# Attention on one core: power and cube of VectorE's exponentials added by a DMA into one tile, two value terms in place of three

## The chip, the core and the metric

The kernel runs on one core of one Trainium2 chip. The metric is device time in microseconds (us) of one execution. The engines are named as in the profile: PE (TensorE's matmuls) and PEld (its weight loads), DVE (VectorE), ACT (ScalarE), POOL (GpSimd), SP (SyncE, which only issues DMAs here). Each takes its instructions in the order in which they were written, and waits at the first one whose data isn't there.

## The reference

Multi-query attention: 8 batches, 1024 positions, 16 heads of 64 for the queries, and one head of keys and values that all 16 share.

```python
scores = np.matmul(q, k.transpose(0, 1, 3, 2)) / np.sqrt(head_dim)
weights = np.exp(scores - np.max(scores, axis=-1, keepdims=True))
weights = weights / np.sum(weights, axis=-1, keepdims=True)
attn_out = np.matmul(weights, v)
```

The kernel subtracts no maximum. It divides by the sum at the end: a column of constants stands beside the 64 columns of v, so the value matmul gives the sum of weights as its 65th column.

## The kernel before

**Units.** The work is cut into 1024 units. A unit is one pair of heads, one half (512) of the queries and one chunk of 128 keys: 128 partitions (keys) x 2 heads x 512 queries = 128x1024 exponentials. Eight units in a row (all keys of one pair and half) make a block; there are 128 blocks.

**Scores.** `scores` writes a unit's 128x1024 scores with two matmuls into one of three PSUM tiles (`sc`). Keys are scaled so that a score is 1024 times the exponent of two.

**Two ways to the exponentials.** Most units (800, kind "A") go to ACT: `scalar_exp`, one activation, fp16 out into one of 22 tiles (`wt`). The others (224, kind "V") go to DVE, which makes the exponential out of the bits of an fp16 number, in a tile `w3` (in the profile `we`) of three parts of 128x1024:

- `ve_bits` adds the exponent's offset to the score and stores it as int16. Read as fp16, part 1 is the power of two times (1 + fraction), a straight line between powers.
- `ve_mantissa` cuts the mantissa out (m, between 1 and 2); `ve_power` cuts the exponent out into part 0; `ve_square` makes m squared; the product of part 1 and m squared, the cubic piece, goes to part 2. POOL makes the first columns of it (`ve_cube`), DVE the others (`ve_rest`).

The exponential is a sum of the three parts with fixed factors. The sum is never made in the tile: `prep_v` keeps three copies of v (in `vp`), with the factors 1, C0 and C3, and the value matmuls add the three terms in PSUM.

**Values.** A block has 16 groups (4 x 128 queries, 2 heads). For each group, `value` multiplies each unit's weights (128x128, loaded as PE's weights) with v (128x65). `terms_of` gives the order in a group: first one term of all 8 units, then the further terms of the V units. Seven groups share a PSUM bank (`ot`); when it is full, DVE takes the reciprocal of the sums (`inverse`), multiplies (`finish`), and SP stores.

`check` tests the sums' range; where one were outside, a second, general program would run after (it doesn't with these inputs).

**Order.** `plan` writes out the order of everything by hand. It keeps a clock for each engine with fixed costs (`T_MM` for a value matmul, `T_ACT` for an activation, `VE_COST` for DVE's), and a time at which each term is `ready`; it emits scores when a PSUM tile is free, values in between, chooses the kind of each unit, and splits each cube between POOL and DVE. `DEFER`, `REST`, `MINC`, `NEXT`, `LATE`, `VE_SLACK` and `NEAR` steer these choices. Only the order reaches the chip. POOL also issues the casting loads of q and v (`load_q`, `load_v`); SP issues q's transposes (`turn_q`) 20 scores later.

Of the kernel before, what the change touches and what calls it, by code (L numbers as in the profile page):

```python
# [11 lines left out]
FP16 = mybir.dt.float16  # L12
I32 = mybir.dt.int32
I16 = mybir.dt.int16
ALU = mybir.AluOpType
# [3 lines left out]

SUM_LO = 128.0  # L20
SUM_HI = 60000.0
C0 = 0.9833984375
C3 = 0.163818359375
CS = 2.1471603163479376
N_WT = 22
N_W3 = 8
N_M = 2
N_M2 = 3
T_PAIR = 214.0
T_IN = 96.0  # L30
T_OUT = 106.0
T_MM = 29.6
T_SCORE = 480.0
T_ACT = 917.0
ACT_DONE = 1110.0
MM_DONE = 270.0
VE_TAIL = 115.0
# [3 lines left out]
GP_COL = 1.887  # L41
GP_TAIL = 230.0
T_LOAD = {"load_q": 640.0, "load_v": 1000.0}
SIDE = (("prep_k", 58), ("prep_v", 72))
VE_COST = {
    "bits": 1141.0,
# [8 lines left out]
    "finish": 542.0,  # L55
}
ORDER = {"bits": 0, "inverse": 1, "finish": 2}
NEXT = {"bits": 0.0, "inverse": 0.0, "finish": 0.0}
MINC = 128
REST = 768  # L60
LATE = 500.0
VSLOT = 1
DEFER = 12
HOLD = 1400.0
VE_SLACK = 2500.0
V_END = 12
RATE = 0.235
NEAR = 2000.0
WAIT = -100.0
T_BITS = 1255.0  # L70
SAFE = 300.0


@with_exitstack
def attention_main(ctx, tc, q, k, v, out, flag):
# [11 lines left out]
    nc = tc.nc  # L87
    B, S, H, D = q.shape
    P = 128
    NKT = S // P  # L90
# [13 lines left out]
    consts = ctx.enter_context(tc.tile_pool(name="consts", bufs=1))  # L104
# [12 lines left out]
    ident16 = consts.tile([P, P], FP16, name="ident16")  # L117
    ones = consts.tile([P, 1], FP32, name="ones")
    rec_all = consts.tile([P, NG], FP32, name="rec_all")
    vps = [consts.tile([P, 3, NKT, 72], FP16, name=f"vp{i}") for i in range(2)]  # L120
    ok_all = consts.tile([P, B + GRP], FP32, name="ok_all")
    qf = consts.tile([P, NKT, P], FP32, name="qf")

# [1 line left out]
    ve = {}  # L125
# [5 lines left out]
    wt = {}  # L131
# [115 lines left out]

    def prep_v(b):
        vp = kv[b]["vp"]
        for i, ci in ((1, C0), (2, C3)):  # L250
            x = nc.vector.tensor_scalar(  # L251
                out=vp[:, i, :, 0:D], in0=vp[:, 0, :, 0:D], scalar1=ci, scalar2=None, op0=ALU.mult
            )
        return x
# [23 lines left out]
    def ve_bits(u, i):  # L278
        p, c, j = where(u)
        w3 = w3p.tile([P, 3, 2, QCH], FP16, tag=f"w3_{i}", name=f"we{p}_{c}_{j}")  # L280
        wt[u] = [(w3[:, 1], 0), (w3[:, 0], 1), (w3[:, 2], 2)]
        ve[u] = {"w3": w3}
        nc.vector.tensor_scalar(  # L283
            out=w3[:, 1].bitcast(I16),
            in0=sc.pop(u),
            scalar1=15.0 * 1024,
            scalar2=0.0,
            op0=ALU.add,
            op1=ALU.max,
        )  # L290

    def ve_mantissa(u, i):
        ve[u]["m"] = mp.tile([P, 2, QCH], FP16, tag=f"m{i}", name=f"m{u}")
        return nc.vector.tensor_scalar(  # L294
            out=ve[u]["m"].bitcast(I16),
            in0=ve[u]["w3"][:, 1].bitcast(I16),
            scalar1=0x3FF,
            scalar2=0x3C00,
            op0=ALU.bitwise_and,
            op1=ALU.bitwise_or,  # L300
        )

    def ve_power(u):
        return nc.vector.tensor_scalar(  # L304
            out=ve[u]["w3"][:, 0].bitcast(I16),
            in0=ve[u]["w3"][:, 1].bitcast(I16),
            scalar1=0x7C00,
            scalar2=None,
            op0=ALU.bitwise_and,
        )  # L310

    def ve_square(u, i):
# [18 lines left out]
    def after_vector(x, key):  # L331
        tc.add_manual_dep(
            x.ins,
            made[key].ins.name,
            mybir.DependencyInfo(mybir.DependencyClass.Sync, mybir.DependencyReason.DATA),
            reason="GpSimd reads beside VectorE's next pass over PSUM",
        )

    def cube_of(u):
        w3 = ve[u]["w3"]  # L340
# [119 lines left out]
    kinds = {}  # L460

    def terms_of(h):
        us = range(h * NKT, (h + 1) * NKT)
        own = [(u, 0) for u in us]
        return own + [(u, i) for i in (1, 2) for u in us if kinds[u] == "V"]

    def plan():
        ops = []
# [4 lines left out]
        t_pe = t_ve = t_act = t_gp = 0.0  # L473
        mode = "v"
        u = 0
# [3 lines left out]
        ready = {}  # L479
# [5 lines left out]
        m2_used = [0.0] * N_M2  # L485
# [5 lines left out]
        behind = None  # L491
        t_behind = 0.0
        loads = []
        live = {}
        h = g = n = 0
        terms = None
# [25 lines left out]
        def share(s):  # L522

            nonlocal t_gp, lock, behind
            if behind is None:
                return
            v = next((v for v in left if left[v]), None)
            if v is not None:
                gs = max(t_gp, t_behind + GP_START, squared[v] + GP_START)
                n = min(int((s - gs - GP_FIX) / GP_COL) // 32 * 32, left[v])  # L530
                if n >= MINC:
                    lo = 2 * QCH - left[v]
                    emit(gs, "cube", v, lo, lo + n, behind)
                    left[v] -= n
                    lock = gs + GP_FIX + n * GP_COL
                    t_gp = lock + GP_TAIL
                    ready[v, 2] = max(ready.get((v, "g"), 0.0), t_gp)
                    ready[v, "g"] = ready.pop((v, 2))
                    for x in loads:
                        emit(t_gp, *x)  # L540
                        t_gp += T_LOAD[x[0]]
                    loads.clear()
            behind = None

        def vector_step(limit):

# [3 lines left out]
            for x in [(r, "bits", v, 0) for v, r in todo] + evict:  # L550
                r, what = x[:2]
                s = max(t_ve, r, min(w3_used) if what == "bits" else 0.0)
# [14 lines left out]
            if not urgent and (  # L567
                chain or left and (flush or left[next(iter(left))] <= REST or u - next(iter(left)) > DEFER)
            ):
                what, v = chain[0] if chain else ("rest", next(iter(left)))  # L570
                old = next(iter(left), None)
                if old is not None and (
                    left[old] <= REST
                    or what == "square"
                    and min(m2_used) == float("inf")
                    or u - old > DEFER
                ):
                    what, v = "rest", old
                s = t_ve
                if what == "mantissa":  # L580
                    s = max(s, ready[v, 0], min(m_used))
                elif what == "square":
                    s = max(s, live["s", v], min(m2_used))
                elif what == "rest":
                    s = max(s, squared[v] + VE_TAIL)
                if s >= limit:
                    return False
                share(s)
                s = max(s, lock)
                if what == "rest":  # L590
                    n = left.pop(v)
                    done = 0.0
                    if n:
                        emit(s, "rest", v, 2 * QCH - n)
                        t_ve = s + VE_FIX + n / 1.92
                        done = t_ve + VE_TAIL
                        behind, t_behind = ("rest", v), t_ve
                    ready[v, 2] = m2_used[live.pop(("m2", v))] = max(done, ready.get((v, "g"), 0.0))
                    return True
                chain.pop(0)  # L600
                t_ve = s + VE_COST[what]
                if what in ("prep_k", "prep_v", "check"):
                    emit(s, what, v)
                    behind, t_behind = (what, v), t_ve
                    return True
                done = t_ve + VE_TAIL
                behind, t_behind = (what, v), t_ve
                if what == "mantissa":
                    live["m", v] = hold(m_used, s)[0]
                    live["s", v] = done  # L610
                    emit(s, what, v, live["m", v])
                elif what == "power":
                    emit(s, what, v)
                    ready[v, 1] = done
                else:
                    m_used[live.pop(("m", v))] = done
                    live["m2", v] = hold(m2_used, s)[0]
                    emit(s, what, v, live["m2", v])
                    left[v] = 2 * QCH
                    squared[v] = t_ve  # L620
                return True
            if best is None or best[1] >= limit:
                return False
            _, s, x = best
            r, what, g0, nn = x
            if what == "bits":
                v = g0
# [3 lines left out]
                t_ve = s + VE_COST["bits"]  # L631
# [64 lines left out]
        while h < H or u < STEPS:  # L696
            guard += 1
            assert guard < 400000

            while vector_step(t_pe):  # L700
                pass
# [55 lines left out]
            idle += 20.0  # L757
        while vector_step(float("inf")):
            pass
        assert u == STEPS  # L760
        return [(what, args) for _, _, what, args in sorted(ops, key=lambda x: x[:2])]

# [18 lines left out]
    with tc.manual_schedule():  # L781
# [6 lines left out]
        for c in range(NKT):  # L788
            load_q(0, c)
        for t in vps:  # L790
            for i, ci in enumerate((1.0, C0, C3)):
                nc.gpsimd.memset(t[:, i, :, D : D + 1], ci)
        nc.vector.tensor_copy(out=ident16, in_=ident)
        nc.vector.memset(ones, 1.0)
# [13 lines left out]
        for c in range(NKT):  # L808
# [6 lines left out]
            "power": ve_power,  # L815
            "square": ve_square,
            "cube": ve_cube,
            "rest": ve_rest,
            "load_q": load_q,
            "load_v": load_v,  # L820
# [140 lines left out]
```

## Time and profile before

| | |
|---|---|
| median of 3 runs | 762.9 us (762.39 to 763.02) |
| profiled execution, its own time | 762.94 us |
| its span, first to last instruction | 761.1 us |
| granted PE clock, mean | 0.997 |
| DMA, mean | 97 GB/s |

The profile gives one execution. Busy time is a union of rows, and rows of one engine overlap: an activation's row takes 1046 ns on average while 800 of them take 745.0 us together. So what an instruction costs its engine is read from the distance between starts, and what an engine lacks from the idle time before its groups. Matmul ends are modelled.

### The profile page before, as it was taken

The page shows a single profiled execution, that of the slowest core. Times are in us where ns is not written, and L with a number is a line of the kernel's source. Part 1 is how long each engine was busy: PE and PEld are TensorE (multiplying, and loading weights), DVE is VectorE, ACT ScalarE, POOL GpSimd, SP SyncE. Part 2 cuts the span into 40 slices and gives each one's busy share as a digit, 9 for nine tenths or more (in the row PEclk, how much of TensorE's full clock was granted, in tenths as well). Part 3 has the DMA queues.
Part 4 walks back from the last instruction along what each step waited for, and adds up shares of the span by engine and source line. Part 5 has one row for each costly group of instructions (what it writes and reads, how often), then busy time and mean ns, then how long its engine had stood idle before and what let it go on. Part 6 is the DMA issues. An engine that isn't in the chain of part 4 may idle for free.

```text
span 761.1 us, 31746 instructions
## 1 busy us (share of the span) xinstructions
PE 746.3 (98%) x13858; PEld 480.7 (63%) x13858; DVE 728.8 (96%) x1474; ACT 747.5 (98%) x803; POOL 327.2 (43%) x364
## 2 busy tenths in 40 slices
PE   6999999999999999999999999999999999999996
PEld 3566666666666666666666666666666665666665
DVE  4999999999999999999999999999999999999994
ACT  7999999999999999999999999999999999999995
POOL 4644444443444344543444344434444334444440
PEclk9999999999999999999999999999999999999999
DMA  9964437663466525665446563467535565211112
GB/s 173 167 121 99 99 64 114 113 117 94 78 118 113 105 62 112 106 113 92 79 93 112 114 113 74 90 111 125 99 75 95 100 112 96 71 44 58 30 58 73
DMA packets 168926, 73.91 MB, mean 97 GB/s; under 512 B 94032, under 2 KB 161616, under 8 KB 168784
## 3 DMA queue, kind: packets, MB, share of 16 engines
q1 hardware_dynamic: 149152, 53.76, 32.7%
q0 software_dynamic: 18576, 17.57, 18.3%
q8 instruction: 109, 1.79, 1.1%
q10 hardware_dynamic: 1056, 0.52, 0.2%
q14 instruction: 33, 0.27, 0.1%
HBM read 37.75 MB, written 33.55 MB: 94 GB/s over the span
## 4 chain that ended last, share of the span: by engine, by line
ACT 54%; PE 42%; issue 3%; DMA 1%; DVE 1%
ACT wt L276 54%; PE ot L396 24%; PE sc L263 17%; DMA knat<-in_k_dram 0%; PE otl L420 0%; DMA out_dram<-osb 0%; DVE osb L354 0%; PE kps L200 0%; PE qps L216 0%; DVE k L191 0%; DVE rec_all L345 0%; DVE k2t L212 0%; PE cnt L837 0%; DVE okm L835 0%; DVE ok_all L443 0%
## 5 line engine op out<-in xcount | busy, mean ns | idle before, releaser
L276 ACT ACTIVATE wt<-sc 128x1024 f16<-128x1024 f32 x800 | 745.0, 1046 | 1.1 <-PE sc L263 0.9
L319 POOL TENSOR_TENSOR we<-we,mm 128x448 f16<-128x448 f16 (+4 forms) x279 | 281.9, 1010 | 409.2 <-DVE mm L315 214.4
L396 PE MATMUL ot<-vp,wt 128*128 128x65 f16 x6336 | 432.2, 194 | 0.0
L396 PE MATMUL ot<-vp,we 128*128 128x65 f16 x5376 | 432.2, 194 | 0.0
L396 PEld LDWEIGHTS <-wt 128*128 128x128 f16 x6336 | 317.4, 97 | 115.0 <-issue 115.0
L396 PEld LDWEIGHTS <-we 128*128 128x128 f16 x5376 | 316.1, 97 | 104.5 <-issue 103.4
L263 PE MATMUL sc<-qt,k2t 64*128 64x512 f16 x2048 | 354.3, 385 | 4.4 <-ACT wt L276 2.9
L283 DVE TENSOR_SCALAR we<-sc 128x1024 int16<-128x1024 f32 x224 | 272.5, 1217 | 8.7 <-PE sc L263 6.7
L315 DVE TENSOR_TENSOR mm<-m 128x1024 f16<-128x1024 f16 x224 | 151.8, 678 | 0.0
L263 PEld LDWEIGHTS <-k2t 64*128 64x128 f16 x2048 | 80.1, 93 | 48.5 <-issue 7.8
L294 DVE TENSOR_SCALAR m<-we 128x1024 int16<-128x1024 int16 x224 | 92.5, 413 | 0.2
L304 DVE TENSOR_SCALAR we<-we 128x1024 int16<-128x1024 int16 x224 | 92.5, 413 | 0.0
L354 DVE TENSOR_TENSOR osb<-ot,rec_all 128x448 f32<-128x448 f32 x146 | 89.2, 611 | 0.2
L327 DVE TENSOR_TENSOR we<-we,mm 128x576 f16<-128x576 f16 (+7 forms) x222 | 87.4, 394 | 0.0
L166 POOL DMA_DIRECT2D q<-in_q_dram x64 | 38.6, 606 | 5.5 <-issue 1.5
L345 DVE RECIPROCAL rec_all<-ot 128x7 f32<-128x7 f32 x146 | 28.7, 197 | 7.4 <-PE ot L396 6.8
L149 POOL DMA_DIRECT2D vp<-in_v_dram x8 | 7.2, 899 | 0.0
L251 DVE TENSOR_SCALAR vp<-vp 128x512 f16<-128x512 f16 x16 | 3.8, 279 | 2.2 <-DMA vp<-in_v_dram 2.2
L200 PE MATMUL kps<-ident,k 128*64 128x128 f16 x16 | 1.3, 314 | 4.4 <-DVE k L191 4.3
L234 DVE TENSOR_SCALAR k16d<-knat 128x1024 f16<-128x1024 f32 x7 | 4.7, 672 | 0.0
L229 DVE COPY qt<-qps 128x512 f16<-128x512 f16 (+1 forms) x2 | 1.1, 555 | 3.0 <-PE qps L216 3.0
L200 PEld LDWEIGHTS <-k 128*64 128x64 f16 x16 | 0.8, 158 | 4.6 <-DVE k L191 4.6
(30 smaller groups left out, 23.7 us busy)
## 6 DMA issues: line engine op xcount, KB each, us to landing
out_dram<-osb SPq DMA_DIRECT2D x109, 256.0 KB, 2.6
q<-in_q_dram POOLq DMA_DIRECT2D x56, 256.0 KB, 4.4
out_dram<-osb SPq DMA_DIRECT2D x38, 128.0 KB, 2.4
knat<-in_k_dram SPq DMA_DIRECT2D x7, 256.0 KB, 3.9
q<-in_q_dram POOLq DMA_DIRECT2D x8, 192.0 KB, 8.2
vp<-in_v_dram POOLq DMA_DIRECT2D x8, 128.0 KB, 5.8
qt<-q SPq DMA_TRANSPOSE x64, 4.8
qf<-in_q_dram ACTq DMA_DIRECT2D x2, 256.0 KB, 4.0
```

The lines of the kernel that those rows point to most:

```text
L166: nc.gpsimd.dma_start(out=q16[(b, c)], in_=q[b, c * P : (c + 1) * P, h0:, :].rearrange("p h d -> p (h d)"),)
L263: nc.tensor.matmul(sc[u][:, hh, :], k2t[r : r + 64, j * P : (j + 1) * P], qt[b][r : r + 64, p % HP, c * QCH : (c + 1) * QCH], start=True, ...
L276: nc.scalar.activation(out=w, in_=sc.pop(u), func=EXP, scale=escale, bias=math.log(CS))
L283: nc.vector.tensor_scalar(out=w3[:, 1].bitcast(I16), in0=sc.pop(u), scalar1=15.0 * 1024, scalar2=0.0, op0=ALU.add, op1=ALU.max,)
L294: return nc.vector.tensor_scalar(out=ve[u]["m"].bitcast(I16), in0=ve[u]["w3"][:, 1].bitcast(I16), scalar1=0x3FF, scalar2=0x3C00, op0=ALU.b ...
L304: return nc.vector.tensor_scalar(out=ve[u]["w3"][:, 0].bitcast(I16), in0=ve[u]["w3"][:, 1].bitcast(I16), scalar1=0x7C00, scalar2=None, op0 ...
L315: return nc.vector.tensor_tensor(out=ve[u]["m2"], in0=m, in1=m, op=ALU.mult)
L319: x = nc.gpsimd.tensor_tensor(out=wu[:, lo:hi], in0=we[:, lo:hi], in1=mm[:, lo:hi], op=ALU.mult)
L327: return nc.vector.tensor_tensor(out=wu[:, lo:], in0=we[:, lo:], in1=mm[:, lo:], op=ALU.mult)
L345: nc.vector.reciprocal(out=rec_all[:, g0 : g0 + n], in_=o[:, 0:n, D])
L354: nc.vector.tensor_tensor(out=ob[:, i0 : i0 + n, :], in0=o[:, 0:n, 0:D], in1=rec.unsqueeze(2).broadcast_to([P, n, D]), op=ALU.mult,)
L396: nc.tensor.matmul(ots[g0][:, gg - g0, 0 : D + 1], w[:, hh, qb * P : (qb + 1) * P], kv[h // (HP * NCH)]["vp"][:, ci, u % NKT, 0 : D + 1], ...
```

## The change

Parts 0 and 2 get the same factor, so that they can be added. The mantissa is cut out with exponent bits 0x3800 in place of 0x3C00 (m between a half and 1, so the cube is a quarter of what it was); the power gets two low bits set (0x0201) by a second operation of the same instruction. A new step, `merge`, issues a DMA from POOL that adds part 0 into part 2 within SBUF. Value terms of a V unit are then part 1 with v times KAPPA, and part 2 with v. `prep_v` makes one scaled copy of v, not two.

`plan` gets the step: a merge is due when power, rest and cube are done, costs POOL 650 ns (`T_MERGE`), and its term is ready 5000 ns after its start (`MERGED`). Several of the planner's costs and choices have other values too. In the built order 220 units go to DVE and 804 to ACT.

```diff
-C0 = 0.9833984375
-C3 = 0.163818359375
-CS = 2.1471603163479376
+KAPPA = 1.5258396029178207
+CS = 3.2766468288976904
-T_PAIR = 214.0
+T_PAIR = 215.5
-T_OUT = 106.0
-T_MM = 29.6
+T_OUT = 120.0
+T_MM = 30.2
-T_ACT = 917.0
+T_ACT = 905.0
+T_MERGE = 650.0
+MERGED = 5000.0
+TERMS = (2,)
-NEXT = {"bits": 0.0, "inverse": 0.0, "finish": 0.0}
-MINC = 128
-REST = 768
-LATE = 500.0
+NEXT = {"bits": 100.0, "inverse": 0.0, "finish": 60.0}
+MINC = 256
+REST = 640
+LATE = 2500.0
-DEFER = 12
+DEFER = 6
-VE_SLACK = 2500.0
+VE_SLACK = 1800.0
-NEAR = 2000.0
+NEAR = 200.0
-SAFE = 300.0
+SAFE = 0.0
-    vps = [consts.tile([P, 3, NKT, 72], FP16, name=f"vp{i}") for i in range(2)]
+    vps = [consts.tile([P, 2, NKT, 72], FP16, name=f"vp{i}") for i in range(2)]
...
-        for i, ci in ((1, C0), (2, C3)):
+        for i, ci in ((1, KAPPA),):
...
-        wt[u] = [(w3[:, 1], 0), (w3[:, 0], 1), (w3[:, 2], 2)]
+        wt[u] = [(w3[:, 1], 1), None, (w3[:, 2], 0)]
...
-            scalar2=0x3C00,
+            scalar2=0x3800,
...
-            scalar2=None,
+            scalar2=0x0201,
             op0=ALU.bitwise_and,
+            op1=ALU.bitwise_or,
...
+    def merge(u):
+        w3 = ve[u]["w3"]
+        nc.gpsimd.dma_start(out=w3[:, 2], in_=w3[:, 0], accum_op=ALU.add)
...
-        return own + [(u, i) for i in (1, 2) for u in us if kinds[u] == "V"]
+        return own + [(u, i) for i in TERMS for u in us if kinds[u] == "V"]
...
+        def merge():
+            nonlocal t_gp
+            done, v = merges.pop(0)
+            s = max(t_gp, done)
+            emit(s, "merge", v)
+            t_gp = s + T_MERGE
+            ready[v, 2] = s + MERGED
...
-                    ready[v, 2] = m2_used[live.pop(("m2", v))] = max(done, ready.get((v, "g"), 0.0))
+                    done = max(done, ready.get((v, "g"), 0.0), ready[v, 1])
+                    m2_used[live.pop(("m2", v))] = done
+                    merges.append((done, v))
...
+            while merges and max(t_gp, merges[0][0]) < min(t_pe, t_ve):
+                merge()
...
-            for i, ci in enumerate((1.0, C0, C3)):
+            for i, ci in enumerate((1.0, KAPPA)):
```

More of the change, by code (lines that the diff above doesn't have):

```diff
@@ L493, in plan @@
         loads = []
+        merges = []
         live = {}
@@ L759, in plan @@
             pass
+        while merges:
+            merge()
         assert u == STEPS
@@ L817, in attention_main @@
             "cube": ve_cube,
+            "merge": merge,
             "rest": ve_rest,
```

## Prediction

> **What bounds the kernel now.** I read the totals, the groups by line, the waits, then the timeline of PE and the chain of waits.
>
> ```profile
> span 761.1 us, 31746 instructions
> PE 746.3 (98%) x13858; PEld 480.7 (63%) x13858; DVE 728.8 (96%) x1474; ACT 747.5 (98%) x803; POOL 327.2 (43%) x364
> ...
> L276 ACT ACTIVATE wt<-sc 128x1024 f16<-128x1024 f32 x800 | 745.0, 1046 | 1.1 <-PE sc L263 0.9
> L396 PE MATMUL ot<-vp,wt 128*128 128x65 f16 x6336 | 432.2, 194 | 0.0
> L396 PE MATMUL ot<-vp,we 128*128 128x65 f16 x5376 | 432.2, 194 | 0.0
> L263 PE MATMUL sc<-qt,k2t 64*128 64x512 f16 x2048 | 354.3, 385 | 4.4 <-ACT wt L276 2.9 <-DVE we L283 0.8
> ```
>
> Three engines are within 4% of the span, so busy shares don't choose. The idle column does: PE never waits before a value matmul, and 4.4 us before all scores. The timeline of PE shows what its time is made of (start, length, group, count):
>
> ```profile
> 403.88 0.39 PE L263 MATMUL sc<-qt,k2t 64*128 64x512 f16 x2
> 404.20 0.20 PE L396 MATMUL ot<-vp,wt 128*128 128x65 f16 x1
> ...
> 404.70 0.19 PE L396 MATMUL ot<-vp,we 128*128 128x65 f16 x1
> 404.83 0.39 PE L263 MATMUL sc<-qt,k2t 64*128 64x512 f16 x2
> ```
>
> 17 values start between 404.20 and 404.70 (31 ns apart), the next score 0.13 us later, the first value 0.32 us after a score. Over the trace from 15 us on, starts lie 31.1 ns apart from value to value (10963 times), 130 from value to score (741), 315 from score to value (741), 223 from one unit's score to the next (262): 737 us in all, with some 4 us over the floors. PE works without a pause and sets the pace.
>
> ACT looks as full, but isn't. The chain of waits (start, length) has it when its scores are ready early, and when they aren't:
>
> ```profile
> 14.67 12.61 ACT wt L276 x14
> ...
> 504.10 4.66 ACT wt L276 x5
> 508.75 0.04 issue
> ```
>
> 12.61/14 is 0.90 us each; 4.66/5 is 0.93. The starts agree: the closest are 903 to 904 ns apart (209 of 799), the mean is 931.5. So 28 ns of each exponential is waiting for PE, hidden inside its row.
>
> DVE: its rows, start to start where nothing is idle, are 1137 ns (bits), 334 (mantissa), 333 (power), 602 (square), 364 (a rest of 576 columns), 116 and 535 (inverse, finish), 726.3 us for all it issues. The other 34.8 us of the span are 10.3 idle in the first 15 us, 11.9 in the middle, 10.1 in the last 16, and 2.5 of row tails. It is nearly full too.
>
> **The change, part by part.**
>
> *Value matmuls.* The two built orders have 11712 before and 9888 after: 1824 fewer (one term for 220 units of 8 matmuls for each head, and four units that go from DVE to ACT). Switches between scores and values stay (744 before, 746 after), so each removed matmul is worth 31.1 ns: 56.7 us. PE alone would then end at 704.4. This is on the path until the next engine binds.
>
> *Who is next: ACT.* It gets 804 exponentials for 800. The first starts at 7.0, the last starts at 751.3 and leaves some 8.7 us after its end. Span = 15.7 + 804 x pitch: at 0.903, never waiting, 741.7; at the old 0.9315, 764.6. The four extra cost 3.6 us by themselves.
>
> *Who is next: DVE.* 220 chains for 224 take away 4 x 2406 ns = 9.6 us; prep_v loses 8 operations x 0.2 = 1.6; the rests are 220 for 222, but longer on average (123 of 576 columns for 87; 22 of 224): +3.6 by their row distances. The power's second operation is free: the mantissa (two operations) and the power (one) both take 413 ns. Sum 718.7, 7.6 less. With the same 34.8 us beside it 753.5; without the 11.9 in the middle 741.6. Those pauses were mostly waits for PE (6.7 us bits for scores, 6.8 us inverse for values), which has time now; but three queues in fixed order, two of them full, won't mesh perfectly. I keep two thirds of the 11.9: 749.6 us. ACT's pitch is then 0.913, a third of its waiting left.
>
> *POOL.* The 213 cubes take some 250 us (279 took 281.9: the 59 of 128 columns are gone). 220 merges are added. Nearest rows for an issue:
>
> ```profile
> L166 POOL DMA_DIRECT2D q<-in_q_dram x64 | 38.6, 606 | 5.5 <-issue 1.5
> L149 POOL DMA_DIRECT2D vp<-in_v_dram x8 | 7.2, 899 | 0.0
> ```
>
> 0.61 to 0.90 us each; 128 rows of 2 KB are the q load's form, so 0.61: 134 us. POOL goes to about 57%. In POOL's queue the merge waits for its unit's rest and stands ahead of the next unit's cube and some q loads. That cube waits for a mantissa, a power and a square behind the rest (1.27 us), so a merge of up to 0.9 us hides; a longer one delays cubes by the excess. A q load's transpose comes 20 scores (14.6 us) later and covers it.
>
> *The merge's landing.* Only PE waits for it: the load of the merged tile for the block's first group, behind which stand the block's 16 groups and all later scores. In the built order it is used 14 to 21 scores (mean 17.9) after the unit's own score, at 0.716 us each ((749.6 - 16) / 1024; the first and last scores stand 16 us from the ends). The order of DVE puts the end of the rest 4.7 us after the bits start (8.2 before: deferral is cut), plus 0.67 from score to bits. Unit by unit that leaves the merge 5.8 us or less in the tightest twentieth, 7.3 at the median. The trace has no adding DMA; rows to bound it:
>
> ```profile
> q<-in_q_dram POOLq DMA_DIRECT2D x56, 256.0 KB, 4.4
> ...
> k2t<-k16d SPq DMA_TRANSPOSE x7, 2.7
> ```
>
> 2.7 us (SBUF to SBUF) to 8.1 (slowest q load in the steady part); I take 4.4: same size, same queue. So nothing is added to the path, but the tight ones have only 1.4 us of cover to spare.
>
> *DMA engines.* They stand at 18.3 + 32.7 + 1.1 + 0.2 + 0.1 = 52.4%, 399 us. One q row of 2 KB out, 4 KB in takes 173 ns (median packet). A merge is 8 such rows on each engine, 1.38 us; 220 of them 304 us: 703 of 750, 94%. The mean q packet is 245 ns, so part of the 399 is already queueing, and the true load is below this. From below: a 512-byte packet takes 27 ns, so a plain 2 KB row 108, and all merges 190 us (79%). I take 173.
>
> Sum: 749.6 span. The profiled run took 762.94, 1.84 more than its span, and the median run 762.9. Forecast 751.5.
>
> **Rivals.**
>
> *Slower: the merge's traffic fills the DMA engines, and the landing goes past its cover.* If an adding row costs two plain rows, it takes 216 ns: 380 us + 399 = 779 us of work for each DMA engine, more than the run has. Landings then grow until PE waits for them. Checked by the loop: a score can't be made before the merge of the unit some 17.9 scores earlier has landed, so pitch = (0.67 + 4.7 + landing)/17.9; it passes today's 0.728 ((761.1 - 16) / 1024) at 7.6 us. At 8.1, the slowest row, it is 0.754, and 1024 x 0.754 + 16 is a span of 788, a time of 790; the 779 us of traffic, with the first 15 us free of merges, give about the same. Decides from 199 ns a row ((750 - 399)/220/8). For: shares of 55 to 60% between 20 and 560 us already (the table of stretches), and q packets of 1.1 us in the worst hundredth. Against: the cast row reads 4 KB in 173 ns, below 199, and part of the share is waiting. Chance 0.17.
> [...] No run here shows an adding DMA.
>
> *POOL's issues stretch beside DVE.* Every merge comes just when DVE does mantissa and power. Q issues that met such passes for 0.4 us took 0.66 on average, 0.74 at most, against 0.59 free. At 0.74 nothing changes; if the pass shut POOL out altogether, 0.6 + 0.67 = 1.27 us just fills the slot before the next cube, and later ones run into DVE's rest; each 0.05 us that a unit so loses on DVE is 220 x 0.05 = 11 us, and 0.02 to 0.04 give 756 to 760. Chance 0.11.
> [...]
>
> *Nothing: the gain is eaten.* ACT's pitch at 0.927 or more (761.4 and up) although PE has 45 us to spare. That needs scores to be late for another reason, all along. Chance 0.04.
>
> **How the numbers follow.** The forecast, with DVE's pauses from none (ACT's floor) to all of them (753.5 + 1.8), is 743.5 to 755.5: 0.66. With the stretched issues, 0.11, faster by over 0.2% (1.5 us, about what a measurement of this kernel can tell from no change) has 0.77. Same 0.04. Slower 0.19: the full DMA engines, and 0.02 for pauses beyond the old ones. The range starts at ACT's floor, 741.7 + 1.8 = 743.5, and reaches over stretched issues to no change, 763; only the 0.19 of slower is left out.
>
> **What would show it.** Right: ACT's mean distance at about 0.913, value matmuls 9888, PE with idle time before scores (waits for ACT and DVE), DVE above 96%, merges landing in 4 to 6 us, no wait of PE for a merge of note. Wrong: PE's weight loads waiting for the merge DMA, merge packets over 199 ns, a DMA share near 100%, or POOL's merge rows over 0.9 us with cubes beside DVE's rests.

## The result: slower by 7.5%, and the profile after

The changed kernel takes 822.46 us (median of 4 executions, 815.82 to 829.41) for 762.96 us of the kernel before measured beside it (762.39 to 764.09): a ratio of 1.0749, 95% interval 1.0678 to 1.082. The forecast was 751.5 us, with a range of 743.5 to 763.0. The ratio leaves out the execution of 829.41 us, which is over 1.5% above the fastest. The profiled execution took 815.82 us.

The totals, the DMA queues and the groups by line of the kernel after (busy time and share, count; packets, MB and share of the 16 engines' span; then busy time, mean ns | idle before, what ended it):

```profile
span 814.1 us, 28859 instructions
...
PE 729.8 (90%) x12034; PEld 447.5 (55%) x12034; DVE 727.2 (89%) x1448; ACT 748.9 (92%) x807; POOL 490.0 (60%) x516
...
q0 software_dynamic: 50256, 75.25, 56.8%
q1 hardware_dynamic: 149152, 53.76, 33.1%
...
L278 ACT ACTIVATE wt<-sc 128x1024 f16<-128x1024 f32 x804 | 746.4, 1110 | 52.3 <-PE sc L265 51.1
L403 PE MATMUL ot<-vp,we 128*128 128x65 f16 x3520 | 377.6, 196 | 49.6 <-DMA we<-we 44.8
...
L344 POOL DMA_DIRECT2D we<-we x220 | 192.8, 876 | 197.0 <-issue 72.5
L285 DVE TENSOR_SCALAR we<-sc 128x1024 int16<-128x1024 f32 x220 | 266.7, 1212 | 33.7 <-PE sc L265 33.1
```

No engine is full any more. The idle columns say who waits for whom: PE, which never waited before a value matmul, now does so for the merge's DMA (44.8 us), and ACT and DVE wait for PE's scores behind it (51.1 and 33.1 us). The waits of the kernel after, by the waiting line (total us, times, longest), show how such time is made up:

```profile
ACT wt L278 <- PE sc L265: 51.1, 65, 2.9
PE ot L403 <- DMA we<-we: 44.8, 37, 3.2
...
DVE rec_all L352 <- PE ot L403: 34.4, 33, 3.2
DVE we L285 <- PE sc L265: 33.1, 33, 4.2
```

37 waits, 1.2 us on average, 3.2 at most. One of them in the timeline of PE of the kernel after (start, length, group, count, idle before):

```profile
184.43 0.61 PE L265 MATMUL sc<-qt,k2t 64*128 64x512 f16 x4
...
185.48 0.39 PE L265 MATMUL sc<-qt,k2t 64*128 64x512 f16 x2
187.95 0.19 PE L403 MATMUL ot<-vp,we 128*128 128x65 f16 x1 [2.07 <-DMA we<-we]
...
189.37 1.04 PE L265 MATMUL sc<-qt,k2t 64*128 64x512 f16 x4
```

PE stops at the first value matmul of a merged tile for 2.07 us. The last line shows an aftermath: four score matmuls take 1.04 us, which took 0.61 us at 184.43. The granted clock is 0.51 between 188.6 and 192.0 us, and 1.00 after that.

From the start times of PE's matmuls: ahead of values of DVE's tiles there are 57 pauses of over 0.1 us more than the usual distance, 57.3 us together (the profile puts 37 of them down to the DMA, the others to POOL's cube or to no one). 46 of them, with 54.7 us, stand at the first use of a merged tile, and the 25 distances of over 1 us hold 45.5 us. ACT's distances tell the same: 593 of 803 lie at 904 to 909 ns, its floor, and the long ones lift the mean to 992.

How the merges land, in the view of line L344 of the kernel after:

```profile
L344 POOL DMA_DIRECT2D we<-we x220: 834/871/1195, 19.7 to 795.2; - x110
...
DMA to landing us min/median/max: 3.2/4.6/8.8
```

The median landing, 4.6 us, is close to the 4.4 that I took. The pauses belong to the upper end: the 25 merges ahead of a distance of over 1 us took 6.8 us on average to land (all 220: 4.8).

### The profile page after: what moved, and what is told of

It reads as the page before. It is cut to its first block, busy times and chain, and to the rows that moved or that the text cites. A ratio compares the mean times of both kernels' runs of the same rounds, so it can differ in the third digit from the quotient of the medians.

```text
span 814.1 us, 28859 instructions
## 1 busy us (share of the span) xinstructions
PE 729.8 (90%) x12034; PEld 447.5 (55%) x12034; DVE 727.2 (89%) x1448; ACT 748.9 (92%) x807; POOL 490.0 (60%) x516
## 3 DMA queue, kind: packets, MB, share of 16 engines
q0 software_dynamic: 50256, 75.25, 56.8%
q1 hardware_dynamic: 149152, 53.76, 33.1%
## 5 line engine op out<-in xcount | busy, mean ns | idle before, releaser
L278 ACT ACTIVATE wt<-sc 128x1024 f16<-128x1024 f32 x804 | 746.4, 1110 | 52.3 <-PE sc L265 51.1
L403 PE MATMUL ot<-vp,we 128*128 128x65 f16 x3520 | 377.6, 196 | 49.6 <-DMA we<-we 44.8
L403 PE MATMUL ot<-vp,wt 128*128 128x65 f16 x6368 | 409.8, 196 | 0.0
L265 PE MATMUL sc<-qt,k2t 64*128 64x512 f16 x2048 | 373.4, 398 | 23.2 <-ACT wt L278 20.4
L403 PEld LDWEIGHTS <-we 128*128 128x128 f16 x3520 | 261.7, 99 | 133.7 <-issue 117.1
L322 POOL TENSOR_TENSOR we<-we,mm 128x448 f16<-128x448 f16 (+4 forms) x213 | 252.0, 1183 | 105.8 <-DVE mm L318 72.7
L344 POOL DMA_DIRECT2D we<-we x220 | 192.8, 876 | 197.0 <-issue 72.5
L285 DVE TENSOR_SCALAR we<-sc 128x1024 int16<-128x1024 f32 x220 | 266.7, 1212 | 33.7 <-PE sc L265 33.1
L318 DVE TENSOR_TENSOR mm<-m 128x1024 f16<-128x1024 f16 x220 | 149.2, 678 | 0.1
L265 PEld LDWEIGHTS <-k2t 64*128 64x128 f16 x2048 | 90.7, 94 | 80.2 <-issue 36.3
L330 DVE TENSOR_TENSOR we<-we,mm 128x576 f16<-128x576 f16 (+6 forms) x220 | 96.1, 437 | 0.2
## 6 DMA issues: line engine op xcount, KB each, us to landing
q<-in_q_dram POOLq DMA_DIRECT2D x8, 192.0 KB, 7.5
```

Source lines behind the costliest of these rows:

```text
L265: nc.tensor.matmul(sc[u][:, hh, :], k2t[r : r + 64, j * P : (j + 1) * P], qt[b][r : r + 64, p % HP, c * QCH : (c + 1) * QCH], start=True, ...
L278: nc.scalar.activation(out=w, in_=sc.pop(u), func=EXP, scale=escale, bias=math.log(CS))
L285: nc.vector.tensor_scalar(out=w3[:, 1].bitcast(I16), in0=sc.pop(u), scalar1=15.0 * 1024, scalar2=0.0, op0=ALU.add, op1=ALU.max,)
L318: return nc.vector.tensor_tensor(out=ve[u]["m2"], in0=m, in1=m, op=ALU.mult)
L322: x = nc.gpsimd.tensor_tensor(out=wu[:, lo:hi], in0=we[:, lo:hi], in1=mm[:, lo:hi], op=ALU.mult)
L330: return nc.vector.tensor_tensor(out=wu[:, lo:], in0=we[:, lo:], in1=mm[:, lo:], op=ALU.mult)
```

## The experiments

The edits are made to the changed kernel.

**The merge written aside.** The same DMA, the same bytes and the same order, but into the part that PE doesn't read, so that PE waits for no landing.

```diff
-        nc.gpsimd.dma_start(out=w3[:, 2], in_=w3[:, 0], accum_op=ALU.add)
+        nc.gpsimd.dma_start(out=w3[:, 0], in_=w3[:, 2], accum_op=ALU.add)
```

> The DMA adds the cube into the power's part instead of the other way round, so its issue, its place in the order and its traffic stay, but PE reads a part that the DMA doesn't write and no longer waits for its landing (the power is left out of the output's sum). Late landing (my theory): the pauses before a V unit's second term go (some 57 us in the trace of after), ACT is left at 904 ns a unit, the clock is back near 1.0, time 745 to 760. Traffic and POOL's issues as the cause: 810 to 825 as after, with the pauses elsewhere. Planner's other choices as the cause: 800 or more too.

Measured: 793.27 us, ratio 1.0393 (1.0341 to 1.0445), and four executions far apart: 771.29 to 809.14. My 745 to 760 missed. Taking the wait away brings 29 us at the medians (822 to 793), and the slowest execution lies below the fastest of the kernel after (815.82). But 793 is still 30 above the kernel before, so something in it costs time without anybody waiting for the landing.

**No merge at all.** The same order without the DMA.

```diff
-        nc.gpsimd.dma_start(out=w3[:, 2], in_=w3[:, 0], accum_op=ALU.add)
+        return
```

> The same order without the adding DMA at all (the power is left out of the sum). Late landing: the same as with the DMA turned aside, 743 to 757, at most 5 us below it. Traffic and POOL's issues: 743 to 757 here, but 810 and more with the DMA turned aside. Planner's other choices: 800 or more.

Measured: 756.98 us (756.57 to 758.67), ratio 0.9925 (0.9908 to 0.9941). The totals and groups of the kernel without the merge:

```profile
span 754.8 us, 28022 instructions
...
PE 710.5 (94%) x12034; PEld 442.8 (59%) x12034; DVE 720.2 (95%) x1448; ACT 740.7 (98%) x807; POOL 292.6 (39%) x296
...
L278 ACT ACTIVATE wt<-sc 128x1024 f16<-128x1024 f32 x804 | 738.2, 1202 | 2.6 <-PE sc L265 2.2
...
L265 PE MATMUL sc<-qt,k2t 64*128 64x512 f16 x2048 | 364.8, 387 | 33.9 <-ACT wt L278 30.5
```

ACT is idle for 2.6 us and PE waits 30.5 us for it: the bound has moved from PE to ACT, as forecast. The span is 59.3 us below that of the kernel after, for 57.3 us of pauses there: the loss goes with these waits. That the two figures are so close is partly chance. In the kernel after, ACT's distances exceed 904 ns by 71 us in all (13 here). 45 us of that stand in distances in which PE pauses by over 0.3 us, and 17 us in 43 distances without such a pause, in stretches in which the granted clock was a half. So ACT loses somewhat less than the pauses, and the slower PE after them adds to it.

**The merge aside, with tiny rows.** As the first, but 64 bytes of each row: all 220 issues stay, and 8 KB of 256 move.

```diff
-        nc.gpsimd.dma_start(out=w3[:, 2], in_=w3[:, 0], accum_op=ALU.add)
+        nc.gpsimd.dma_start(out=w3[:, 0, 0, 0:32], in_=w3[:, 2, 0, 0:32], accum_op=ALU.add)
```

> As the DMA turned aside, but each of its 128 rows moves 64 bytes in place of 2048 (the power is left out of the sum): the same count of descriptors, the same POOL issues, nearly no bytes. If what was left with the DMA turned aside (790 for 757 without it) is bytes on the DMA engines (weight-load and instruction fetches, q, stores all queue behind merges): 755 to 762. If it is POOL's issues beside DVE: 780 or more.

Measured: 757.48 us (757.01 to 758.12), ratio 0.9923 (0.9907 to 0.994), the time of no merge. Its view of line L344:

```profile
L344 POOL DMA_DIRECT2D we<-we x220: 845/912/1195, 19.2 to 736.8; - x110
```

The issues are as long as in the kernel after (912 for 871 ns), and cost nothing that shows. What costs time with the merge written aside is its bytes. (The expectation names weight loads among what these could hold up; no DMA issue of the profile feeds those.)

**Half the merge.** One of the two heads of a unit; PE waits for it as for the whole.

```diff
-        nc.gpsimd.dma_start(out=w3[:, 2], in_=w3[:, 0], accum_op=ALU.add)
+        nc.gpsimd.dma_start(out=w3[:, 2, 0], in_=w3[:, 0, 0], accum_op=ALU.add)
```

> The merge proper, for one of the two heads only (the other head's power is left out of the sum): PE waits for it at the same place in the order, 110 of 220 merges' bytes are gone. If the landing grew because the DMA engines are full: landing median under 4, slowest tenth under 5, pauses before merged tiles under 15 us in all, 755 to 775. If the fixed part of a landing (3.2 us at least, and 0.5 before the issue) and the short lead cause the pauses alone: 795 or more.

Measured: 771.1 us (768.9 to 775.21), ratio 1.0117 (1.0085 to 1.0148). The DMA issues and the queue of this kernel (KB each, median us to landing; packets, MB, share):

```profile
q0 software_dynamic: 50256, 46.42, 42.6%
...
we<-we POOLq DMA_DIRECT2D x220, 128.0 KB, 3.5
```

As many issues and the same leads, with half the bytes: the landing's slowest tenth begins at 5.4 us (6.6 in the kernel after; I had expected under 5), and 10.6 us of pauses are left of 57.3. A shorter transfer and a lower load of the DMA engines act together here; this run doesn't part them.

**The merge aside, once more.** A second profile of the first experiment, since its executions lay so far apart.

> The same kernel as the first with the DMA turned aside, for a second profile: its times spread from 771 to 809 and the one profiled was at the low end. If PE's blocks of 256 instructions, fetched by the same DMA engines, are what is late when nobody waits for a merge: every pause of PE of 1.5 us and more ahead of a weight load that waits for nothing falls on the same place modulo 256 as in the first (193), and they make up most of what the run is above 757. If q's transposes or stores are late: pauses at a batch's first scores.

Measured: 807.84 us (one execution), span 806.1, 51 us above the order without a merge, with nobody waiting for a merge. The waits of this kernel, and one in the timeline of PE:

```profile
ACT wt L278 <- PE sc L265: 48.7, 36, 8.9
...
PE ot L403 <- issue: 18.4, 5, 8.8
...
PE sc L265 <- issue: 14.6, 4, 5.2
```

```profile
689.30 0.20 PE L403 MATMUL ot<-vp,wt 128*128 128x65 f16 x1
698.25 0.29 PE L403 MATMUL ot<-vp,wt 128*128 128x65 f16 x2 [8.75 <-issue]
```

"issue" is a wait for nothing that the profile shows as a semaphore. PE stands still for 8.75 us in front of an ordinary value matmul. Counting PE's rows from the start of the trace, this one is number 20673 = 80 x 256 + 193. Nine pauses in the steady part are longer than 1.4 us. Seven of them (1.7 to 8.9 us, 28.7 in all) stand at 193 modulo 256, and so do all three in the first experiment's profile (3.0, 1.7 and 4.7 us). No loop of the kernel has a period of 256 rows; by their count, the packets of the instruction queue have:

```profile
q8 instruction: 94, 1.54, 0.8%
```

94 packets of 16384 bytes for PE's 24,109 rows: about 256 rows a packet, and so some 64 bytes a row (an estimate from these counts). In each of the ten pauses such a packet is under way, and PE goes on 1.2 to 1.5 us after its end (here it ends at 696.79). So, by these times, PE's next block of instructions came late, through a queue that the profile lists among those of the 16 DMA engines. (This is argued: a packet of q8 doesn't name the instructions in it.) It is the start that is late, more than the transfer that is long: this packet takes 2.1 us, but begins 12.5 us after PE has passed row 193 of the block before. It ends 14.6 us after that; in the order without a merge a packet does so after 3.5 us at most, in the kernel after, after 5.3 at most. There PE reaches row 193 never less than 3.3 us after the packet: blocks come sooner, PE, which stops for merges, comes later, and no pause stands at a block. The other two long pauses (5.3 and 2.3 us) are waits for q's transposes, in the view of line L178 of the kernel aside:

```profile
  PE sc L265: 7.2, 2
...
DMA to landing us min/median/max: 3.9/7.2/30.0
```

A transpose takes up to 30.0 us to land there (9.6 in the kernel after); one issued at 298.0 landed at 305.79, and PE's scores went on at 305.88. Blocks and transposes make 36 of the 51 us. The other 15 are in shorter distances, and ACT's show where: 14 us of what they exceed 904 ns by stand in 29 distances in which PE doesn't pause, in stretches in which the granted clock was a half.

**Longer leads.** If waits for the landing are the loss, the planner should be told of a longer landing, and put the merged term later.

```diff
-MERGED = 5000.0
+MERGED = 6500.0
```

> Only MERGED is changed, 5000 to 6500, so that the planner puts the use of a merged tile later: mean lead 19.2 scores for 18.1, the fewest 16 for 14; 227 V units for 220. Late landing: most pauses go (landings of 6.5 us and more were the last tenth), 755 to 780. Traffic: 805 to 825. Planner's other choices: 805 to 825.

> MERGED 8000: mean lead 20.0, nearly all 18 or more; 236 V units, 788 for ACT. Late landing: nearly no pause for a merge, ACT's floor would be 15.7 + 788 x 0.904 = 728 but DVE has 16 chains more (38 us), so DVE sets the pace: 745 to 770. Traffic: 805 to 825.

Measured: 803.49 us with 6500 (ratio 1.0474, 1.0435 to 1.0514) and 825.46 with 8000 (1.08, 1.0725 to 1.0876). The pauses at DVE's tiles shrink as expected, from 57 to 25 and 14 us, but both times miss what I expected of late landing (755 to 780, 745 to 770), and the second is no faster than the kernel after. Two runs divide that: 8000 without the DMA, and 8000 with 220 units on DVE again (`RATE` 0.219; it had given DVE 236, with 788 exponentials on ACT).

> The order made with MERGED 8000, without the DMA (the power is left out of the sum). If that order's 825 came from its own pauses (22 wt tiles held longer, 236 chains on DVE): 795 or more here too. If it came from merges: 755 to 775.

> MERGED 8000 and RATE 0.219 in place of 0.235: 220 V units as in after, mean lead 19.4 scores for 18.1. Lead alone: pauses before merged tiles under 20 us, 775 to 795 (what bytes cost stays). If the order with long leads is slow by itself: 805 or more.

Measured: 798.46 us without the DMA (two executions; ratio 1.0457, 1.0436 to 1.0478) and 817.17 with 220 units (1.0661, 1.0596 to 1.0727). In the first, the groups of scores and exponentials:

```profile
L278 ACT ACTIVATE wt<-sc 128x1024 f16<-128x1024 f32 x788 | 733.1, 1068 | 48.8 <-PE sc L265 47.1
...
L265 PE MATMUL sc<-qt,k2t 64*128 64x512 f16 x2048 | 360.3, 387 | 79.9 <-ACT wt L278 70.5
```

With no merge in it, that order has ACT idle for PE and PE idle for ACT. (Why is only argued: values that come later hold the tiles of scores and exponentials longer.) A longer lead is bought with a worse order; 8000 costs 41 us before a byte moves (798 for 757).

**Fewer merges.** Only V units at the first places of a block are merged, whose term is used latest; the others keep three terms. First the places 0 to 3 (110 merges), then the same with `MERGED` 6500 (113), then the places 0 to 2 (85).

```diff
+    def joined(u):
+        return u % NKT < 4
...
-        return own + [(u, i) for i in TERMS for u in us if kinds[u] == "V"]
+        return own + [(u, i) for i in (1, 2) for u in us if kinds[u] == "V" and (i == 2 or not joined(u))]
...
```

> Complete computation: only V units in the first half of their block (110 of 219) are merged, the others keep three terms with the new factors. Half the bytes, 896 value matmuls fewer than before in place of 1824 (28 us of PE, still more than ACT can use). If the full DMA engines are the cause: share 70 to 78%, landing median under 4.3, pauses at merged tiles under 10 us, 757 to 768. If a merge costs whatever its bytes: 785 or more.

> The same with MERGED 6500: 113 merges, mean lead 19.8 scores. Full DMA engines: 755 to 768, pauses at merged tiles nearly none; the longer lead may cost pauses of its own order, as with 8000. A merge costs whatever its bytes: 785 or more.

> Complete computation: V units at places 0 to 2 of their block only, 85 merges, most with a lead of 20 scores; 680 value matmuls fewer than before (21 us of PE), as much as ACT can use. Full DMA engines: share 65 to 72%, 755 to 763, below the kernel before by up to 1%. A merge costs whatever its bytes: 775 or more.

Measured: 777.14 us (ratio 1.0172, 1.0155 to 1.0189; my 757 to 768 missed), 765.55 (1.0014, 0.9992 to 1.0036) and 765.04 (1.0011, 0.9996 to 1.0026; expected 755 to 763). Half the merges with leads mostly of 16 to 18 scores still make PE wait, in the groups of the first of the three:

```profile
L278 ACT ACTIVATE wt<-sc 128x1024 f16<-128x1024 f32 x805 | 740.6, 1233 | 22.3 <-PE sc L265 22.3
...
L403 PE MATMUL ot<-vp,we 128*128 128x65 f16 x4376 | 401.6, 195 | 18.6 <-DMA we<-we 17.3
```

With leads of about 20 scores most of the loss is gone, but so is the gain: PE has 856 and 1080 more matmuls than in the kernel after (739.7 and 743.4 us busy, where the order without a merge has 710.5), so what a late landing costs it can hardly make up. None of the versions that compute the whole result beats the kernel before.

## Why the prediction was wrong, step by step

**Value matmuls, and ACT as the next bound: right.** 9888 value matmuls, as counted. (A block has 8 groups, 4 x 128 queries of 2 heads, where the texts ahead say 16, and a term of a unit is 8 matmuls, 4 for each head; the 1824 come out the same.) Without the merge the order runs at 757.0 us, 5.5 above the forecast, and slightly faster than before (0.9925). ACT's floor of 904 ns is where 593 of its 803 distances lie even in the kernel after. The term for what ACT still waits was too small: I kept a third of its old waiting (a pitch of 0.913); without the DMA it is (754.8 - 15.7)/804 = 0.919, somewhat over half. The 749.6 itself came from DVE, less a third of its 11.9 us of pauses; DVE's idle time (span less busy) is 34.6 us without the merge and was 32.3 before, so no pause of its went away.

**POOL: wrong in size, right in effect.** An issue takes 0.87 us (834 to 1195 ns), the v load's price, not the q load's 0.61. It also starts 0.58 us on average after the end of its unit's rest (0.30 at least), where I had none. That the next cube hides it was right: 220 issues with tiny rows cost 0.5 us. With that the rival of stretched issues falls. Its 1.27 us for an issue, with POOL shut out altogether, was a supposition that the kernel after does not show: no issue there took longer than 1195 ns, and a cost in time was not visible.

**The row and the share: right.** A merge's packet of 2 KB takes 178 ns (median) for the 173 taken. The queues add up to 56.8 + 33.1 + 1.1 = 91.0% of the span, 741 us, for 703 forecast; stretches with a share above 1 (below) show that this counts packets that wait. The first rival's price of two plain rows, 216 ns, was a supposition that no run shows: 178 is 1.65 times the 108 that I estimated for a plain row.

**The merge's landing: the step that failed.** It said that nothing is added to the path. Two things were wrong in it.

First, the chain from score to landing had gaps left out. Forecast: 0.67 to the bits, 4.7 to the end of the rest, 0 to the issue, 4.4 to land, 9.8 us. Measured means: 1.01, 5.16, 0.58 and 4.82, 11.6 us. Only 0.4 us of the difference is the landing; 0.6 is POOL's start, and 0.8 the parts ahead, in which the pauses themselves have a share.

Second, a median was set against a cover that each of 220 merges has to meet. I had a cover of 5.8 us or less for the tightest twentieth, 7.3 at the median, and knew a spread of 2.7 to 8.1. With the first 1.4 us (0.34 + 0.46 + 0.58) taken off, the cover is 4.4 to 5.9, and the landing's slowest tenth lies above 6.6. That is enough for 48 of 220 merges to be used within 0.2 us of landing. And since ACT and DVE have hardly any slack by the prediction's own count, little of this is made up: 57.3 us of pauses, 59.3 us of span, of which a part is PE at half the clock after a pause, for which the prediction had no term.

**The first rival: its mechanism happened, its condition did not.** I let it decide from 199 ns a row, where the DMA engines would have more work than time. It came at 178 ns. Transfers were held up all the same: a store of 256 KB, which the change doesn't touch, lands in 3.9 us (median) in the kernel after and in 2.6 before. The table of stretches of the kernel after (the last three numbers: granted clock, DMA share, GB/s) has

```profile
20.00:200.00 180.00, 165.15 (x2671) 100.69 (x2667) 167.50 (x330) 171.77 (x186) 114.82 (x119) 0.96 1.03 179
200.00:380.00 180.00, 162.73 (x2744) 100.43 (x2740) 167.39 (x331) 168.47 (x183) 114.29 (x119) 0.97 0.94 165
```

The mean landing is 4.8 us here, 3.8 with half the bytes and 3.1 with tiny rows, but these transfers differ in size too. With merges of full size and half as many of them (the first of the runs with fewer merges, queues at 72%) the mean is 4.5, and the slowest tenth still begins at 6.3. So the share alone doesn't make the slow tail; what else is under way goes with it. In the kernel after, the 86 merges issued with no q load and no transpose of q in flight took 4.0 us on average to land, the 40 with both in flight 6.1, and 13 of the 24 over 6.6 us are among these 40. No run moved those transfers, so that they are the cause is not shown.

I had used the share as a threshold, full or not, and given 0.17 to a case that the 94% I had myself worked out spoke for. Its price, a pitch for all units, was also another: 790 us, where single pauses made it 822.

**What the prediction did not see at all:** with the wait taken away, the merge's bytes still cost some 36 us at the median (793 for 757). Late blocks of PE's instructions stand for 9.4 of the 14.7 us that the first profile of that version lies above the order without a merge, and for 28.7 of 51.3 in the second; late transposes of q stand for another 7.6 there, and PE at half the clock for most of the rest. No run took either cause away alone, so their sizes rest on where the pauses stand. It also means that the 36 us are not part of the 59 of the kernel after: there no pause stands at a block, and PE waits for merges instead. That blocks would be late if the merges landed in time is argued from the version aside.

## What to carry to other kernels

A transfer that comes back onto the critical path is to be costed by its slow tail against the smallest cover, not by its median. Here a tenth of the landings took over 6.6 us with the queues at 91%, and over 6.3 at 72%, and 16 of the 24 slowest were issued while a load of q was in flight. With three engines within 4% of the span in the kernel before, such waits were hardly made up: 57.3 us of pauses, 59.3 us of span. And under such a load PE also stood for what no line of the program issues: in two profiles of the version aside (DMA shares of 0.88 to 1.14 by stretch), by the place of the pauses, for its instruction blocks, for as long as 8.9 us.

## What the runs showed of the hardware

- In the second profile of the version aside the instruction queue (q8, 0.8% of the 16 DMA engines' span) brought 94 packets of 16 KB for PE's 24,109 rows, about 256 rows a packet, and the ten pauses of the two profiles stood at one place modulo 256. PE went on 1.2 to 1.5 us after the packet's end. With the merge's traffic and no wait for it (DMA shares of 0.88 to 1.14 by stretch) such a pause was as long as 8.9 us; in the order without a merge no such packet took over 1.8 us (2.7 with the traffic), and PE never stood for one.
- About half of the pauses of over 1 us in the kernel after were followed by PE at half pace: value matmuls 56 ns apart in place of 31. Between 40 and 800 us the granted clock was a half in 12 stretches of 3.4 or 6.8 us, each of which began during such a pause or at most 1.6 us after it, and in none between 40 and 750 us in the order without a merge. The mean granted clock was 0.960 for 0.997 before. Some pauses of 1.5 to 2.1 us were followed by such a stretch, and others weren't.
- In the kernel after, POOL started the issue of a merge 0.30 us or more after the end of its unit's rest on DVE, in 172 of 220 cases some 0.5 us after it. The issue took 0.87 us (median) with rows of 2 KB and 0.91 with rows of 64 bytes.
